# An mLSTM, attention and PEER block on one core: the mLSTM's branch product moved into the attention, and tiles made ahead spread differently

## The chip, the cores and the metric

The kernel runs on one core of a Trainium2 chip. The core has a tensor engine for matrix products (TensorE, PE), a vector engine (VectorE, DVE), a scalar engine for activations (ScalarE, ACT), GpSimd (POOL), and SyncE (SP), whose queue issues most DMA transfers. Each engine works through its own queue in a fixed order and waits on semaphores for what other engines produce. The metric is the device time of one launch in microseconds (us), taken as the median of several runs.

## The reference

One transformer block for 512 latent tokens of width 1024, with 256 context tokens beside them. What matters here, cut to its core:

```
sh1, sc1, g1, sh2, sc2, g2 = adaLN(c) = silu(c) @ w_ada + b_ada          # 6 x 1024 numbers
h = rms(x) * g * (1 + sc1) + sh1
q, k, v, o, gates, aq, ak, av, G = split(h @ w_in)                       # G: two gates of 1024 columns
m = mlstm(q, k, v, gates over latents and context, both directions)       # 4 heads of 128
m = rms(m) * norm_g * sigmoid(o)                                          # 512 columns
a = window_attention(aq, ak, av, context keys, sink)                      # 8 query heads of 64, 2 kv heads
z = sigmoid(G_m) * (m @ w_branch_m) + sigmoid(G_a) * (a @ w_branch_a)
x = x + g1 * (z @ w_out)
x = x + g2 * peer(rms(x) * g * (1 + sc2) + sh2)                           # 16384 experts, 16 of each of 8 heads
```

All is in float32. The two branch products, the gates G and z @ w_out are the part that the change touches; the PEER part (experts) follows and takes most of the time.

## The kernel before

A float32 product is split in three: each operand becomes a high half (a copy rounded by ACT, `whi`, `hhi`) and a low half (the rest, a subtraction, `wlo`, `hlo`), and `mm3` (L182) issues hi times hi, lo times hi and hi times lo into one PSUM bank (L183 to L185). These are called split matmuls below. A product tile gives 128 output columns for all 512 tokens: with an inner width of 1024 it is 24 split matmuls (a gate, `gate_proj`, L646; an output tile), with 512 it is 12 (a branch product).

The part around the change runs in these stages. The projections of h; the mLSTM cell (L480 to L560) over chunks of 128 tokens in both directions; the attention in four blocks of 128 queries (L592 to L643): for a block the scores of eight heads (L607, L608), a masked maximum on DVE (L615), exponentials on ACT (L619), a scaling on DVE (L626), then for each of four or five key blocks eight transposes of the scores (L632), two copies out of PSUM (`pTs`, L635 on DVE, L637 on ACT) and the product with the values (L640, PV). Then `num`, the result of the mLSTM, is transposed (L670) and scaled to `mt` (L672), and split to `mhi`, `mlo`. Sixteen gate tiles of G (L681 and what it calls) are written to a DRAM tile `sgd`. The branch products of both branches follow for eight column tiles (L687 to L713): load the two gate tiles (`sgm`), load and split the weights (`w_br`), 24 split matmuls, two multiplications, one addition on GpSimd, split into `zhi`, `zlo`. Then the output projection with eight tiles of `w_out` (L740 to L753), the norm, and PEER.

The order is not that of the text. A scheduler of the framework lists the instructions of all these stages by priority and readiness and fixes a queue for each engine; so gates are placed between the attention's short operations. It is bounded by buffers: a pool tag with n buffers makes the next tile wait until an earlier one is released. Tag `SGS` (2 buffers) holds the gates, tag `A` (10 slots, `ga`) the large arrays, tag `B` (9) short-lived tiles, `wraw` (4), `whi` and `wlo` (3) the weights. `ps` are PSUM banks for split products.

Three other streams run beside. `adas` (L138) loads weight rows of the adaLN and reduces each with the vector silu(c) in `silp` on DVE (`dot`, L133, 1024 columns; tile `wada`). `ahead(n)` (L355) prepares n tiles of the PEER weights: load (`sraw`, L358), copy to the high half (`shi`, ACT), subtract in place (DVE, L361), and at its next call store the low half in DRAM (`lows`). There are 36 such tiles, and each call site says how many it makes at once. Lines of the kernel before are used above and in the profile; the changed kernel's lines lie 1 to 40 further on in this part.

## Time and profile before

| | us |
|---|---|
| median of 3 runs | 1827.71 (1825.52 to 1828.05) |
| the profiled execution | 1819.1 |
| its span | 1817.3 |
| PE busy in the span | 1736.9 (96%) |
| DVE busy | 1428.5 (79%) |
| ACT busy | 765.2 (42%) |
| GpSimd busy | 487.1 (27%) |

The span runs from the first to the last instruction of one execution, and the profiled execution's time has some 2 us around it. "Busy" is the time in which an engine executes instructions; a matmul's end is modelled and consecutive matmuls overlap, so a busy PE isn't always one at its peak. [...] An idle time is put down to the engine or transfer whose result came last. The rows are in a section of their own below.

### The profile page before, as it was taken

The page shows a single profiled execution, that of the slowest core. Times are in us where ns is not written, and L with a number is a line of the kernel's source. Part 1 is how long each engine was busy: PE and PEld are TensorE (multiplying, and loading weights), DVE is VectorE, ACT ScalarE, POOL GpSimd, SP SyncE. Part 2 cuts the span into 40 slices and gives each one's busy share as a digit, 9 for nine tenths or more (in the row PEclk, how much of TensorE's full clock was granted, in tenths as well). Part 3 has the DMA queues.
Part 4 walks back from the last instruction along what each step waited for, and adds up shares of the span by engine and source line. Part 5 has one row for each costly group of instructions (what it writes and reads, how often), then busy time and mean ns, then how long its engine had stood idle before and what let it go on. Part 6 is the DMA issues. An engine that isn't in the chain of part 4 may idle for free.

```text
span 1817.3 us, 24986 instructions
## 1 busy us (share of the span) xinstructions
PE 1736.9 (96%) x9079; PEld 1479.7 (81%) x9079; DVE 1428.5 (79%) x2756; ACT 765.2 (42%) x1139; POOL 487.1 (27%) x385
## 2 busy tenths in 40 slices
PE   8999898997998999999989999999999999999998
PEld 4877775664777899999889999999999999988886
DVE  6977977454655999999738888888888888886665
ACT  5452466554445334554523333333333333334332
POOL 0001133210203552000025454445454444420000
PEclk9999998998999999999999999999999999999999
DMA  9466645443795225699999999999989999986662
GB/s 370 136 203 197 210 169 182 176 151 116 244 307 181 82 93 208 250 346 345 325 394 375 343 336 352 350 324 355 367 319 353 350 340 340 372 321 249 234 229 81
DMA packets 154764, 485.09 MB, mean 267 GB/s; under 512 B 15376, under 2 KB 45584, under 8 KB 151568
## 3 DMA queue, kind: packets, MB, share of 16 engines
q1 hardware_dynamic: 91088, 314.39, 47.8%
q0 software_dynamic: 37008, 135.28, 20.4%
q10 hardware_dynamic: 26544, 33.82, 5.3%
q8 instruction: 71, 1.16, 0.3%
q14 instruction: 53, 0.43, 0.1%
HBM read 421.30 MB, written 62.13 MB: 266 GB/s over the span
## 4 chain that ended last, share of the span: by engine, by line
PE 70%; DMA 11%; DVE 10%; ACT 5%; issue 3%; POOL 1%; SPq 0%; ACTq 0%; DVEq 0%; POOLq 0%
PE pa L184 9%; PE pa L185 9%; PE pa L183 9%; PE pu L183 9%; PE pu L185 9%; PE pu L184 9%; DMA Gd<-stg 4%; PE ps L185 3%; PE ps L183 2%; PE ps L184 2%; PE a L640 2%; DMA wada<-in_w_adaT 2%; ACT stg L1024 1%; PE a L632 1%; DVE wada L135 1%
## 5 line engine op out<-in xcount | busy, mean ns | idle before, releaser
L183 PE MATMUL pu<-h2hi,whi 128*128 128x384 f32 (+1 forms) x1152 | 402.3, 349 | 4.7 <-ACT St L1134 3.3
L185 PE MATMUL pu<-h2lo,whi 128*128 128x384 f32 (+1 forms) x1152 | 395.9, 344 | 0.7 <-DVE h2lo L180 0.7
L184 PE MATMUL pu<-h2hi,wlo 128*128 128x384 f32 (+1 forms) x1152 | 395.6, 343 | 0.0
L795 DVE TENSOR_TENSOR wlo<-wraw,whi 128x1024 fp32r<-128x1024 f32 x210 | 256.9, 1224 | 99.0 <-ACT whi L784 97.1
L183 PE MATMUL pa<-whi,wh 128*128 128x512 f32 x768 | 299.8, 390 | 5.5 <-ACT wh L1146 5.5
L184 PE MATMUL pa<-whi,wl 128*128 128x512 f32 x768 | 301.6, 393 | 1.8 <-DVE wl L1150 1.7
L185 PE MATMUL pa<-wlo,wh 128*128 128x512 f32 x768 | 301.1, 392 | 0.0
L784 ACT ACTIVATE whi<-wraw 128x1024 fp32r<-128x1024 f32 x272 | 286.5, 1053 | 28.5 <-PE pa L184 10.8
L1071 POOL DMA_INDIRECT gath<-in_u,idx x128 | 166.3, 1299 | 404.4 <-DMA Sd<-St 228.1
L183 PEld LDWEIGHTS pu<-h2hi,whi 128*128 128x128 f32 x1152 | 218.3, 189 | 13.6 <-ACT St L1134 3.6
L184 PEld LDWEIGHTS pu<-h2hi,wlo 128*128 128x128 f32 x1152 | 218.4, 190 | 7.8
L185 PEld LDWEIGHTS pu<-h2lo,whi 128*128 128x128 f32 x1152 | 218.0, 189 | 6.3 <-DVE h2lo L180 1.1
L1071 POOL DMA_INDIRECT gath<-in_v,idx x128 | 164.3, 1284 | 178.4 <-DVE tokh L1103 163.8
L183 PEld LDWEIGHTS pa<-whi,wh 128*128 128x128 f32 x768 | 144.8, 189 | 34.8 <-ACT wh L1146 6.6
L184 PEld LDWEIGHTS pa<-whi,wl 128*128 128x128 f32 x768 | 144.5, 188 | 32.1 <-DVE wl L1150 3.6
L185 PEld LDWEIGHTS pa<-wlo,wh 128*128 128x128 f32 x768 | 144.6, 188 | 30.2
L1103 DVE SCALAR_TENSOR_TENSOR tokh<-gath,gw,tokh 128x1024 f32<-128x1024 f32 x127 | 163.1, 1284 | 0.6
L1146 ACT ACTIVATE wh<-act 128x384 fp32r<-128x384 f32 x84 | 44.2, 526 | 268.7 <-DVE act L1142 268.7
L1095 DVE CUSTOM_DVE_ANT_0 gath<-gath,tokh 128x1024 f32<-128x1024 f32 x128 | 154.6, 1218 | 2.4 <-DMA gath<-in_u,idx 2.4
L1134 ACT ACTIVATE act<-pu 128x384 f32<-128x384 f32 x84 | 41.3, 492 | 178.3 <-PE pu L185 178.3
L52 POOL TENSOR_TENSOR wlo<-wraw,whi 128x1024 fp32r<-128x1024 f32 x20 | 49.0, 2449 | 234.5 <-ACT whi L51 194.8
L51 ACT ACTIVATE whi<-wraw 128x1024 fp32r<-128x1024 f32 (+1 forms) x60 | 61.6, 1028 | 80.8 <-PE ps L184 29.8
(352 smaller groups left out, 2829.2 us busy)
## 6 DMA issues: line engine op xcount, KB each, us to landing
wraw<-in_uT SPq DMA_DIRECT2D x128, 512.0 KB
wraw<-in_v SPq DMA_DIRECT2D x128, 512.0 KB
Gt<-Gd SPq DMA_DIRECT2D x17, 1536.0 KB
Gd<-stg ACTq DMA_DIRECT2D x24, 1024.0 KB
sraw<-in_uT SPq DMA_DIRECT2D x36, 512.0 KB
lows<-sraw SPq DMA_DIRECT2D x36, 512.0 KB
wlo<-lows SPq DMA_DIRECT2D x36, 512.0 KB
wada<-in_w_adaT SPq DMA_DIRECT2D x32, 512.0 KB
```

The costliest lines, as they stand in the source:

```text
L51: S.activation(hi, src, AF.Copy)
L52: (eng or V).tensor_tensor(out=lo, in0=src, in1=hi.bitcast(F32), op=ALU.subtract)
L183: PE.matmul(p, sh, mh, start=first, stop=False)
L184: PE.matmul(p, sl, mh, start=False, stop=False)
L185: PE.matmul(p, sh, ml, start=False, stop=last)
L784: S.activation(his[j], raws[j], AF.Copy)
L795: (G if pool else V).tensor_tensor(out=los[j], in0=raws.pop(j), in1=his[j].bitcast(F32), op=ALU.subtract)
L1071: G.indirect_dma_start(out=t, out_offset=None, in_=sparse["src"][s // 128], in_offset=bass.IndirectOffsetOnAxis(ap=sparse["idx"][:, s // 1 ...
L1095: V.tensor_tensor_reduce(out=t, in0=t, in1=tokh[:, 0], scale=1.0, scalar=0.0, op0=ALU.mult, op1=ALU.add, accum_out=gw[:, 0, s:s + 1])
L1103: V.scalar_tensor_tensor(out=tokh[:, 1], in0=t, scalar=gw[:, 0, s - 128:s - 127], in1=tokh[:, 1], op0=ALU.mult, op1=ALU.add)
L1134: S.activation(acts[i], p, AF.Gelu_apprx_tanh)
L1146: S.activation(wh, acts[i], AF.Copy)
```

## The change

Four things change together. The mLSTM's transposes and `mt` tiles are moved to stand between the first four and the last four gates of the attention's branch, with `mt` in tag `SGS`, and the branch products of the mLSTM are formed beside their gates (for a pair of column tiles at a time) and multiplied into them before the result goes to DRAM. The halves `ahi`, `alo` of the attention's output are made only behind these products; the outputs of the first three blocks wait in `ao` until then. `ahead` is called once beside each gate and each product up to there, then for every second tile in the attention's product and in the output projection. And silu(c) is copied into the mask's tile at the start of the attention, so that the later dots read it there (the name in the order is then `amask`, not `sil`) and the slot of `sil` comes free earlier. The addition of the two branches moves from GpSimd to DVE.

```diff
--- before.py
+++ after.py
@@ -99,6 +99,7 @@
 
     warm = cst.tile([128, 1], F32, name="warm")
     silp = ga([128, 2, D], F32, "sil")
+    sils = [silp[:, 0], silp[:, 1]]
 
     def silu(i, nm):
         nc.sync.dma_start(silp[:, i], A[nm].to_broadcast([128, D]))
@@ -132,7 +133,7 @@
 
     def dot(w, i, col, keep=False):
         junk = wb([128, D], mybir.dt.bfloat16, "junk") if keep else w
-        V.tensor_tensor_reduce(out=junk, in0=w, in1=silp[:, i], scale=1.0, scalar=0.0,
+        V.tensor_tensor_reduce(out=junk, in0=w, in1=sils[i], scale=1.0, scalar=0.0,
                                op0=ALU.mult, op1=ALU.add, accum_out=col)
 
     def adas(a, b):
@@ -562,7 +563,10 @@
     banks(("m2", "m1"), a1=(2, 1), a2=(2, 2))
     aqt = ga([128, NB, 512], F32, "aqt")
     nc.sync.dma_start(aqt, aqd)
-    amask = ga([128, 640], F32, "amask")
+    amask_ = ga([128, 640 + D], F32, "amask")
+    amask = amask_[:, 0:640]
+    S.activation(amask_[:, 640:], silp[:, 0], AF.Copy)
+    sils[0] = amask_[:, 640:]
     nc.sync.dma_start(amask, A["amask"])
     sink = load_const("sink", [128, 8])
 
@@ -588,7 +592,12 @@
         for o in (a, z):
             V.tensor_tensor(out=kst[g][o, 1], in0=pk[a], in1=kst[g][a, 0].bitcast(F32), op=ALU.subtract)
 
-    ahi, alo = ga([128, NB, 4, 128], F32R, "ahi"), ga([128, NB, 4, 128], F32R, "alo")
+    ao = ga([128, 3, 4, 128], F32, "ao")
+    halves = {}
+
+    def attended(n, src):
+        split(halves["ahi"][:, n], halves["alo"][:, n], src)
+
     for n in range(4):
 
         lat = [b for b in (n - 1, n, n + 1) if 0 <= b < 4]
@@ -639,7 +648,8 @@
             for g in range(2):
                 PE.matmul(po[64 * g:64 * g + 64], akv[:, blk, 128 + 64 * g:192 + 64 * g], pts[g],
                           start=(i == 0), stop=(i == nk - 1))
-        split(ahi[:, n], alo[:, n], po)
+        if n < 3:
+            S.activation(ao[:, n], po, AF.Copy)
         adas(28 + 5 * n, 33 + 5 * n)
 
     def gate_tile(name):
@@ -663,23 +673,54 @@
         gate_proj(cO + h * 128, sigo[:, h])
         ahead(1)
     g_m = load_const("g_mlstm", [128, 4])
+
+    sgd = dr.tile([8, 128, 2, T], F32, name="sgd")
+
+    def branch_gate(n, br):
+        st = gen.tile([128, T], F32, name="sgs", tag="SGS", bufs=2)
+        gate_proj(cG + br * 1024 + n * 128, st)
+        return st
+
+    def branch_weights(br, q):
+        wbr = wp.tile([128, 2, 4, 128], F32, name="wraw", tag="wraw", bufs=WR)
+        nc.sync.dma_start(wbr, A["w_br"][br, q])
+        whi = wp.tile([128, 2, 4, 128], F32R, name="whi", tag="whi", bufs=3)
+        wlo = wp.tile([128, 2, 4, 128], F32R, name="wlo", tag="wlo", bufs=3)
+        split(whi, wlo, wbr)
+        return whi, wlo
+
+    def attention_gates(a, b):
+        for n in range(a, b):
+            nc.sync.dma_start(sgd[n, :, 1], branch_gate(n, 1))
+            ahead(1)
+
+    attention_gates(0, 4)
     mhi, mlo = ga([128, NH, T], F32R, "mhi"), ga([128, NH, T], F32R, "mlo")
     for h in range(4):
-        p = pst([128, T], "a1")
+        p = pst([128, T])
         for b in range(4):
             PE.transpose(p[:, b * 128:b * 128 + 128], num[0][:, b, h, 0:128], ident)
-        mt = wb([128, T], F32, "mt")
+        mt = gen.tile([128, T], F32, name="mt", tag="SGS", bufs=2)
         V.scalar_tensor_tensor(out=mt, in0=p, scalar=g_m[:, h:h + 1], in1=sigo[:, h], op0=ALU.mult, op1=ALU.mult)
         split(mhi[:, h], mlo[:, h], mt)
-
-
-    sgd = dr.tile([8, 128, 2, T], F32, name="sgd")
-    for n in range(8):
-        for br in range(2):
-            st = gen.tile([128, T], F32, name="sgs", tag="SGS", bufs=2)
-            gate_proj(cG + br * 1024 + n * 128, st)
-            nc.sync.dma_start(sgd[n, :, br], st)
+    attention_gates(4, 8)
+    for q in range(4):
+        sts = []
+        for i in range(2):
+            sts.append(branch_gate(2 * q + i, 0))
             ahead(1)
+        whi, wlo = branch_weights(0, q)
+        for i in range(2):
+            p = pst([128, T])
+            for k in range(4):
+                mm3(p, whi[:, i, k], wlo[:, i, k], mhi[:, k], mlo[:, k], k == 0, k == 3)
+            V.tensor_tensor(out=sts[i], in0=p, in1=sts[i], op=ALU.mult)
+            nc.sync.dma_start(sgd[2 * q + i, :, 0], sts[i])
+            ahead(1)
+    for nm in ("ahi", "alo"):
+        halves[nm] = ga([128, NB, 4, 128], F32R, nm)
+    for n in range(4):
+        attended(n, ao[:, n] if n < 3 else po)
 
     V.tensor_tensor(out=mod[:, 16:48], in0=mod[:, 16:48], in1=b_ada[:, 16:48], op=ALU.add)
 
@@ -687,31 +728,21 @@
     banks(("a2", "a1", "ps"), ps=(6, 1), ps2=(1, 2))
     zh = [ga([128, 4, T], F32R, "zhi%d" % i) for i in range(2)]
     zl = [ga([128, 4, T], F32R, "zlo%d" % i) for i in range(2)]
-    for n in range(8):
-        sgs = [wb([128, T], F32, "sgm") for _ in range(2)]
-        for br in range(2):
-            nc.sync.dma_start(sgs[br], sgd[n, :, br])
-        wbr = wp.tile([128, 2, 4, 128], F32, name="wraw", tag="wraw", bufs=WR)
-        nc.sync.dma_start(wbr, A["w_br"][n])
-        whi = wp.tile([128, 2, 4, 128], F32R, name="whi", tag="whi", bufs=3)
-        wlo = wp.tile([128, 2, 4, 128], F32R, name="wlo", tag="wlo", bufs=3)
-        split(whi, wlo, wbr)
-        pz = []
-        for br, (ah, al) in enumerate(((mhi, mlo), (ahi, alo))):
+    for q in range(4):
+        whi, wlo = branch_weights(1, q)
+        for i in range(2):
+            n = 2 * q + i
+            sgs = [wb([128, T], F32, "sgm") for _ in range(2)]
+            for br in range(2):
+                nc.sync.dma_start(sgs[br], sgd[n, :, br])
             p = pst([128, T])
             for k in range(4):
-                if br == 0:
-                    mh, ml = ah[:, k], al[:, k]
-                else:
-                    mh, ml = ah[:, :, k], al[:, :, k]
-                mm3(p, whi[:, br, k], wlo[:, br, k], mh, ml, k == 0, k == 3)
-            pz.append(p)
-        z0 = wb([128, T], F32, "sgm")
-        V.tensor_tensor(out=sgs[0], in0=pz[0], in1=sgs[0], op=ALU.mult)
-        V.tensor_tensor(out=sgs[1], in0=pz[1], in1=sgs[1], op=ALU.mult)
-        G.tensor_tensor(out=z0, in0=sgs[0], in1=sgs[1], op=ALU.add)
-        split(zh[n // 4][:, n % 4], zl[n // 4][:, n % 4], z0)
-        ahead(1)
+                mm3(p, whi[:, i, k], wlo[:, i, k], halves["ahi"][:, :, k], halves["alo"][:, :, k], k == 0, k == 3)
+            z0 = wb([128, T], F32, "sgm")
+            V.tensor_tensor(out=sgs[1], in0=p, in1=sgs[1], op=ALU.mult)
+            V.tensor_tensor(out=z0, in0=sgs[0], in1=sgs[1], op=ALU.add)
+            split(zh[n // 4][:, n % 4], zl[n // 4][:, n % 4], z0)
+            ahead(i)
     g1 = mod[:, 16:24]
     x1T = Pair(F32, T, "x1T")
     x1d = dr.tile([128, 4, D], F32, name="x1d")
@@ -750,7 +781,7 @@
         square(x1T, n, acc, T)
         if n:
             residual_out(n - 1)
-        ahead(1)
+        ahead(n % 2)
     ahead(0)
 
 
@@ -1400,7 +1431,8 @@
     f["sink"] = np.tile(a["attn_sink"][0], (128, 1))
     cut = lambda m: m.reshape(-1, 128, m.shape[1] // 128, 128).transpose(2, 1, 0, 3)
     f["w_gate"] = ct(cut(np.concatenate([f["w_in"][:, 2048:2560], f["w_in"][:, 2832:]], axis=1)))
-    f["w_br"] = ct(np.stack([cut(a["w_branch_m"][0]), cut(a["w_branch_a"][0][hp])], 2))
+    pair = lambda m: cut(m).reshape(4, 2, 128, 4, 128).transpose(0, 2, 1, 3, 4)
+    f["w_br"] = ct(np.stack([pair(a["w_branch_m"][0]), pair(a["w_branch_a"][0][hp])]))
     f["w_out"] = ct(cut(a["w_out"][0]))
     f["w_in"] = ct(f["w_in"][:, 0:2832])
     f["w_q"] = ct(a["peer_w_query"][0].reshape(8, 128, 16, 128).transpose(2, 1, 0, 3).reshape(16, 128, 1024))
```

The queue that the scheduler makes for PE changes most. This is the start of the first attention block's PV before; `a` with a number is a PSUM tile, `hhi`, `hlo` the halves of h, so L183 to L185 are matmuls of a gate:

```order
L183 MATMUL ps<-hhi_212,whi 128x512
L184 MATMUL ps<-hhi_212,wlo 128x512
L185 MATMUL ps<-hlo_214,whi 128x512
L632 MATMUL a_2199<-c_ident,sm 128x128
L183 MATMUL ps<-hhi_211,whi 128x512
L632 MATMUL a_2199<-c_ident,sm 128x128 x2
L184 MATMUL ps<-hhi_211,wlo 128x512
L632 MATMUL a_2199<-c_ident,sm 128x128
L185 MATMUL ps<-hlo_213,whi 128x512
L632 MATMUL a_2206<-c_ident,sm 128x128
L183 MATMUL ps<-hhi_211,whi 128x512
L632 MATMUL a_2206<-c_ident,sm 128x128
```

And the same place now, with all of the block's first two key blocks (L641 are the transposes, L649 the PV, L702 the transposes of `num`):

```order
L641 MATMUL a_2199<-c_ident,sm 128x128 x4
L641 MATMUL a_2206<-c_ident,sm 128x128 x2
L649 MATMUL a_2113<-pTs,akv 64x512
L641 MATMUL a_2206<-c_ident,sm 128x128 x2
L649 MATMUL a_2113<-pTs,akv 64x512
L641 MATMUL a_2215<-c_ident,sm 128x128 x4
L702 MATMUL ps<-c_ident,num_1471 128x128 x4
L641 MATMUL a_2222<-c_ident,sm 128x128 x4
L649 MATMUL a_2113<-pTs,akv 64x512
L702 MATMUL ps<-c_ident,num_1471 128x128 x4
L649 MATMUL a_2113<-pTs,akv 64x512
```

Where three matmuls of a gate stood to every two or three transposes, none stands now; the transposes of `num` came from behind the attention. The next matmul of a gate comes 138 instructions after the eighth gate's last.

On DVE the dots have moved. This is the queue at the start of the mLSTM before (`vL`, `kvc` and `ktok` are copies of values and keys, L135 a dot with its read of the sum):

```order
L135 ISA wada_2457,mod<-wada_2457,sil 128x1024
L135 ISA mod 128x1
L135 ISA wada_2460,mod<-wada_2460,sil 128x1024
L135 ISA mod 128x1
L486 COPY vL<-ps 128x4x128 x2
L135 ISA wada_2631,mod<-wada_2631,sil 128x1024
L135 ISA mod 128x1
L486 COPY kvc<-ps 128x4x128
L493 COPY ktok<-ps 128x512 x4
L135 ISA wada_2634,mod<-wada_2634,sil 128x1024
L135 ISA mod 128x1
```

This is the queue in the PV of the first attention block now (L136 a dot, L704 `mt`, L644 copies of transposed scores):

```order
L136 ISA wada_2628,mod<-wada_2628,amask 128x1024
L136 ISA mod 128x1
L644 COPY pTs<-a_2206 128x512
L704 SCALAR_TENSOR_TENSOR mt<-ps,c_g_mlstm,sigo 128x512
L644 COPY pTs<-a_2215 128x512
L704 SCALAR_TENSOR_TENSOR mt<-ps,c_g_mlstm,sigo 128x512
L362 TENSOR_TENSOR sraw<-sraw,shi 128x1024
L136 ISA wada_2631,mod<-wada_2631,amask 128x1024
L136 ISA mod 128x1
L362 TENSOR_TENSOR sraw<-sraw,shi 128x1024
L136 ISA wada_2634,mod<-wada_2634,amask 128x1024
L136 ISA mod 128x1
```

The dots that stood around the copies of keys and values now stand among the copies that the PV needs, with `mt` and the tiles made ahead.

On SP, whose queue issues the loads, these are the weights of the last branch products before (`sgm` loads a gate back from `sgd`, which a store of `sgs` has written):

```order
L695 DMA wraw<-in_w_br 128x1024
L693 DMA sgm<-sgd 128x512 x4
L355 DMA lows<-sraw 128x1024
L358 DMA sraw<-in_uT 128x1024
L693 DMA sgm<-sgd 128x512 x2
L355 DMA lows<-sraw 128x1024
L695 DMA wraw<-in_w_br 128x1024
L693 DMA sgm<-sgd 128x512 x2
```

And those of the attention's product now:

```order
L718 DMA sgd<-sgs 128x512
L737 DMA sgm<-sgd 128x512
L356 DMA lows<-sraw 128x1024
L718 DMA sgd<-sgs 128x512
L359 DMA sraw<-in_uT 128x1024
L686 DMA wraw<-in_w_br 128x1024
L737 DMA sgm<-sgd 128x512 x2
L359 DMA sraw<-in_uT 128x1024
```

The load of weights (L686) now stands among the stores of the last gated products (L718); before, no store of a gate was left in this place.

## Rows read from the trace of the kernel before

**Rows 1.** Part 1 of the page: busy us, share of the span, instructions

```profile
PE 1736.9 (96%) x9079; PEld 1479.7 (81%) x9079; DVE 1428.5 (79%) x2756; ACT 765.2 (42%) x1139; POOL 487.1 (27%) x385
```

**Rows 2.** busy time of each engine by stage; the first line names the columns

```profile
core 0: us, PE busy (x) PEld busy (x) DVE busy (x) ACT busy (x) POOL busy (x), PEclk, DMA share, GB/s
178.00:187.00 9.00, 3.25 (x21) 2.47 (x20) 7.29 (x12) 1.53 (x2) 1.45 (x1) 0.80 0.84 291
187.00:260.00 73.00, 67.86 (x439) 59.52 (x437) 61.60 (x154) 42.98 (x90) 11.84 (x5) 0.98 0.53 184
260.00:285.00 25.00, 20.33 (x85) 15.84 (x85) 21.52 (x21) 14.98 (x20) 14.11 (x4) 0.86 0.37 133
285.00:343.00 58.00, 55.06 (x251) 37.66 (x251) 36.33 (x81) 39.02 (x64) 12.72 (x6) 0.97 0.49 170
343.00:418.40 75.40, 75.40 (x331) 47.54 (x330) 35.38 (x79) 41.10 (x68) 14.15 (x6) 1.00 0.48 170
418.40:445.00 26.60, 20.50 (x50) 6.90 (x50) 11.02 (x18) 8.18 (x11) 0.00 (x0) 0.68 0.39 140
445.00:450.50 5.50, 2.45 (x17) 1.59 (x17) 4.77 (x8) 2.60 (x5) 0.00 (x0) 1.00 0.44 137
450.50:497.00 46.50, 44.88 (x192) 36.02 (x193) 27.99 (x34) 17.84 (x21) 11.96 (x7) 1.00 0.63 220
497.00:552.00 55.00, 50.18 (x221) 38.58 (x220) 31.45 (x34) 25.65 (x32) 2.95 (x3) 1.00 0.89 305
420.00:435.00 15.00, 12.34 (x26) 4.00 (x26) 8.12 (x12) 5.38 (x7) 0.00 (x0) 0.58 0.54 189
```

**Rows 3.** timeline of PE, 429 to 451: start, us, line, names [idle before, releaser]

```profile
429.81 1.97 PE L640 MATMUL a<-pTs,akv 128*64 128x512 f32 x2
...
434.37 1.12 PE L632 MATMUL a<-c_ident,sm 128*128 128x128 f32 x4
...
450.50 0.47 PE L183 MATMUL ps<-mhi,whi 128*128 128x512 f32 x1 [1.96 <-DVE mt L672]
```

**Rows 4.** timeline of PE, 347 to 349, columns as in rows 3

```profile
347.90 0.60 PE L632 MATMUL a<-c_ident,sm 128*128 128x128 f32 x4
348.43 1.07 PE L640 MATMUL a<-pTs,akv 128*64 128x512 f32 x2
```

**Rows 5.** timeline of PE, 456 to 484, columns as in rows 3

```profile
456.10 0.39 PE L183 MATMUL ps<-mhi,whi 128*128 128x512 f32 x1
...
483.87 0.39 PE L183 MATMUL ps<-mhi,whi 128*128 128x512 f32 x1
```

**Rows 6.** tile wada, 150 to 235: count, ns min/median/max, first and last start

```profile
L135 DVE CUSTOM_DVE_ANT_0 wada<-wada,sil x20: 1205/1221/3471, 150.4 to 218.9; 128x1024 f32<-128x1024 f32 x20
```

**Rows 7.** timeline of PE, 178 to 187, columns as in rows 3

```profile
181.46 1.25 PE L492 MATMUL ps<-c_ident,kT 128*128 128x128 f32 x8 [1.94 <-DVE vL L486]
186.52 0.77 PE L504 MATMUL m<-qT,kT 128*128 128x128 f32 x2 [3.81 <-DVE ktok L493]
```

**Rows 8.** timeline of DVE, 179 to 184, columns as in rows 3

```profile
179.57 1.22 DVE L135 CUSTOM_DVE_ANT_0 wada<-wada,sil 128x1024 f32<-128x1024 f32 x1 [2.36 <-DMA wada<-in_w_adaT]
```

**Rows 9.** groups of DVE, 285 to 445: busy us, mean ns, idle before

```profile
L615 DVE CUSTOM_DVE_ANT_0 sm<-a,amask,c_sink 128x640 f32<-128x640 f32 (+1 forms) x24 | 19.4, 835 | 1.7 <-PE a L608 1.7
L361 DVE TENSOR_TENSOR sraw<-sraw,shi 128x1024 fp32r<-128x1024 f32 x14 | 19.4, 1388 | 18.5 <-ACT shi L360 18.5
L626 DVE TENSOR_SCALAR sm<-sm,mx 128x512 f32<-128x512 f32 (+1 forms) x32 | 16.2, 580 | 0.1
...
L617 DVE TENSOR_SCALAR mx<-mx 128x1 f32<-128x1 f32 x32 | 4.4, 147 | 0.0
```

**Rows 10.** groups of DVE, 450.5 to 552, columns as in rows 9

```profile
L52 DVE TENSOR_TENSOR wlo<-wraw,whi 128x1024 fp32r<-128x1024 f32 x13 | 17.4, 1339 | 8.2 <-ACT whi L51 8.0
...
L52 DVE TENSOR_TENSOR zlo<-sgm,zhi 128x512 fp32r<-128x512 f32 x8 | 5.5, 689 | 11.6 <-ACT zhi L51 11.6
```

**Rows 11.** DMA queues, 497 to 552: packets, MB, share of 16 engines

```profile
q1 hardware_dynamic: 8060, 16.76, 89.2%
```

## The prediction, made before the changed kernel was run

> **What bounds the kernel now.** I read the page's busy shares first: TensorE (PE) is busy 96% of the span [rows 1], so a change pays where PE waits or runs at a low clock, and costs where it opens such a place. Then I cut the stretch the diff touches into its stages and read a table by stage [rows 2]; before 178 us and behind 552 us the instructions stand in the old order, so these 374 us decide. Three of its stages have gaps: 178 to 187 us (PE busy 3.25 of 9), 418.4 to 445 (20.50 of 26.6, granted clock 0.68) and 445 to 450.5 (2.45 of 5.5). From 343 to 418.4 PE is busy all the time at a clock of 1.00: there one split matmul after another of the gates lies between the attention's short chains. [...] So the question for the change is where the 480 split matmuls of this stretch (288 of gates, 192 of products) stand: the price of one is the time from 456.10 to 483.87, which 120 of them fill, 0.2314 us each [rows 5].
>
> **Start of the mLSTM, 178 to 285.** Twenty adaLN dots (VectorE, DVE, 1.22 us each) ran from 150.4 to 218.9 [rows 6]; eleven of them lie behind 178 us. Their weight tiles came early because the vector `sil` held a slot that others wait for; now a copy in the mask's tile serves them, and the order has them late: seven at the end of the mLSTM and thirteen in the first two attention blocks. At the start PE waits 1.94 us for the value copies and 3.81 for the key copies [rows 7]; in front of each stands a dot in DVE's queue, and the first dot waited 2.36 us for its transfer [rows 8]. I take two dots and a third of that wait, -3.2 us (0 to -5.75). From 187 to 260 PE idles 5.1 of 73 and DVE loses its remaining dots: -2 (0 to -5). From 260 to 285 seven dots, 8.5 us, come to a DVE that has 3.5 of 25 free, with PE idle 4.7 already: +2.5 (0 to +8.5). Sum -2.7. The nine dots before 178 stood beside dense matmuls and are counted at nothing.
>
> **First uncovered stretch, 285 to 343.** The four `mt` tiles of the mLSTM now use the two buffers that gates use (tag SGS), ahead of the next gates. The order shows what follows: after the eighth gate (285 us) PE's queue holds no split matmul until the fourth `mt` is made, in the PV of the second block. Before, 128 of them lay there, and PE was busy 55.06 of 58 at 0.97 [rows 2]; these 29.6 us of work go behind. What is left is the serial chain of blocks one and two, as in the old tail. Without cover I price a key block of PV like the tail, 26.6 / 4 = 6.65 us, less the tail's 1.00 us of start shared by four: 6.4. The chain from 285: two dots, two `sraw` subtractions (1.39 each) and eight scalings (0.58 each) with 2 us of exponentials and sums [rows 9], 12 us; four key blocks, 25.6; the scores of block two, eight times 0.835 + 0.147 [rows 9], 7.9; two dots, eight scalings and the small operations, 8.5; one key block, 6.4. Together 60.4 us where 58 stood, and reads of the accumulators on top: +3. The thirteen dots of this stretch are part of it only where they are named; the others lie where DVE waits for PE. Bounds: at a full clock a key block is 2 x 0.60 + 2 x 1.0 and two waits of 0.75, 4.7, or 3.2 if the waits overlap, so five of them save 8.5 to 16; upward, if the other nine dots all add, +11.
>
> [...] The row: with 12.34 of 15 us busy on transposes and PV, PE was granted 0.58 [rows 2]. [...]
>
> **Second block to the end of attention, 343 to 445.** Before: 101.95 us, with 160 split matmuls and the bare tail. Now 186 split matmuls lie there and reach the tail. The tail's own work at a full clock is 8 x 0.60 + 8 x 1.0 = 12.8 us instead of 26.6 (-13.8); 26 more split matmuls add 6.0; the clock must rise first, +1.5 by my estimate from the clock of 0.97 in neighbouring stages. Sum -6.3 (-10 to 0). Of the mLSTM's branch product only two of eight tiles (24 of 96 matmuls) stand beside the attention: the rest stands behind it, which is why the saving isn't larger.
>
> **mt stage, 445 to 450.5.** It goes: its transposes and scalings are in the stretch above. PE's wait of 1.96 us for the last mt goes with it [rows 3]. -5.5; what is late next is the split of the fourth block's output, hidden behind gates.
>
> **Gates and products, 450.5 to 497.** Before: 192 split matmuls, 46.5 us [rows 2]. Now 198 behind the attention (gates of the mLSTM branch with six product tiles) and 96 of the attention's product: 294 x 0.2314 = 68.0, +21.5. This pays for the 128 that left the first stretch.
>
> **Lateness in these stages.** In the last 96 matmuls (22.2 us) DVE has eight multiplications, eight additions that GpSimd did before, eight splits, 0.69 each, with six `wlo` at 1.34 [rows 10] and five `sraw` at 1.39, as [rows 9] have it: 31.6 us. PE can run ahead into the output projection only by the `k` whose halves are made, about 5 us. I take +6.5 (0 to +12). DMA: a round of two gates and two products (72 matmuls, 16.7 us) moves eleven tiles of 512 KB and two of 256, 6.3 MB or 377 GB/s; the row gives 16.76 MB at a share of 89.2% over 55 us, which is 342 at a full share [rows 11]. The 2.75 rounds would take 50.5 us instead of 45.8. The low-half stores can lag, and the loads of weights have four buffers: 0 (0 to +5). In SP's queue the weights of the attention's product now stand behind the stores of the last gated products, which wait for PE; I count that in the 6.5.
>
> [...]
>
> **Output projection, 497 to 552.** 54.7 us against 192 x 0.2314 = 44.4, with `wlo` as what PE waits for. Three ahead tiles instead of six stand there, each a load, a store, 1.22 us of DVE: I take -6 (-9 to 0).
>
> **Sum.** -2.7 + 3 - 6.3 - 5.5 + 21.5 + 6.5 + 0 - 6 = +10.5 against the profiled execution's 1819.1 us (span 1817.3), 1829.6. The runs shown have a median of 1827.71, 8.6 above the profiled execution, so the forecast is 1827.7 + 10.5, some 1838 us. A measurement here tells 0.2% (3.7 us) from no change.
>
> **Rivals.** One: the clock stays up in the bare stretch. For it: between 285 and 343 the clock was 0.97, and the granted clock of 187 to 260 was 0.98 with short operations among the split ones [rows 2]. Against it: the 0.58 of the tail, which has the same instructions. Then the term is -10 instead of +3 (a key block 3.2 to 4.7 instead of 6.4): the sum is -2.5, 1825 us, not slower, with 1822 at its lower end. It decides if the granted clock there is over some 0.85.
> Two: the late stages are bound by DMA and DVE together. For it: 377 GB/s wanted against 342, 31.6 us of DVE beside 22.2 of PE, and a share of 0.89 in the projection behind [rows 2, 11]. Against it: the share of 0.63 in the old products. Lateness becomes 5 + 12 and the sum +21: 1849 us.
> Three: the end overlaps well (lateness 0, projection at -8) and the start gives 6: -6 + 3 - 6.3 - 5.5 + 21.5 - 8 = -1.3, 1826 us, no measurable change. For it: PE needs only the first `k` halves to start the projection; against it: DVE's order is fixed, and seven dots move into the mLSTM's end.
> That the product isn't beside the attention at all is half true by the order (six of eight tiles) and is in the sum.
>
> **How the numbers follow.** Forecast (1832 to 1844) 0.42, rival one 0.20, two 0.18, three 0.20. Faster by over 0.2%: two fifths of rival one and a third of rival three, 0.15. Within 0.2%: the rest of both and a little of the forecast's edge, 0.22. Slower: 0.63. The range goes from rival one's lower part to rival two's middle, 1823 to 1849.
>
> **What would show it.** Right: between 285 and some 345 us a granted clock near 0.6 and PE idle over 10 us, with no `hhi` matmul; a clock of 1.00 through the rest of the attention; no transposes of `num` behind it; the first matmul of the projection some 15 us later than now. Wrong: a first stretch under 52 us (rival one), a last product stage over 34 us or weights waited for from DMA (rival two), a projection under 47 us right behind a 22 us product stage (rival three). A mLSTM that ends later than 285 by over 5 us would mean that the seven dots cost more than I counted.

## The result and the profile after

The changed kernel is slower: 1838.11 us (median of 7 runs) against 1823.53, a ratio of 1.0074 with a 95% interval of 1.0050 to 1.0098. That is +14.6 us where +10.5 was forecast. That the forecast time, 1838 us, was met to within 1 us is luck: with four more runs the median of the kernel before came out 4.2 us lower than the 1827.7 that the forecast started from, and the change 4.1 us larger. The profiled executions (1819.1 and 1837.57 us) lie 4.4 below and 0.5 below these medians, so their spans differ by 18.5 us. Each term can be read in them.

First the table by stage of the changed kernel, columns as in [rows 2]; the bounds are the same places in the program. The clock (column PEclk) is the mean clock granted to PE in a stretch, as a share of its full speed. In the trace of before it was 1.00 from 420 to 422 us and 0.50 from 424 to 438; these two are the upper and the lower level below.

```profile
150.00:176.00 26.00, 26.00 (x121) 21.33 (x121) 5.68 (x19) 6.04 (x12) 4.78 (x2) 1.00 0.25 88
...
176.00:275.10 99.10, 88.32 (x540) 75.27 (x538) 83.89 (x169) 56.67 (x108) 23.59 (x8) 0.98 0.43 151
275.10:334.30 59.20, 42.00 (x149) 22.25 (x150) 49.85 (x108) 27.04 (x52) 7.29 (x3) 0.77 0.58 199
334.30:428.40 94.10, 93.01 (x395) 55.80 (x394) 49.30 (x106) 49.75 (x79) 12.45 (x5) 0.98 0.37 130
...
428.40:483.20 54.80, 48.41 (x199) 37.94 (x198) 22.96 (x21) 22.60 (x25) 9.67 (x4) 0.97 0.79 270
483.20:514.20 31.00, 25.85 (x96) 19.88 (x96) 20.17 (x26) 11.76 (x14) 0.00 (x0) 0.89 0.93 313
514.20:571.20 57.00, 50.03 (x221) 39.98 (x221) 33.04 (x35) 25.37 (x33) 7.14 (x3) 0.97 0.78 266
...
320.00:335.00 15.00, 10.38 (x26) 4.74 (x27) 12.55 (x29) 4.75 (x12) 0.00 (x0) 0.62 0.42 141
```

Beside the stages of before, with what was forecast:

| stage | before us | after us | difference | forecast |
|---|---|---|---|---|
| to the eighth gate (285.05; 275.1) | | | -10.0 | -2.7 |
| bare stretch | 58.2 | 59.2 | +1.0 | +3 |
| rest of the attention | 101.8 | 94.2 | -7.6 | -6.3 |
| mt stage | 5.5 | none | -5.5 | -5.5 |
| product stages | 46.5 | 85.7 | +39.2 | +21.5 and +6.5 |
| output projection to the norm | 56.9 | 57.0 | +0.1 | -6 |
| sum | | | +17.2 | +10.5 |

Then rows with a wait from PE's timeline, columns as in [rows 3].

```profile
179.31 1.13 PE L505 MATMUL m<-qT,kT 128*128 128x128 f32 x8 [1.52 <-DVE ktok L494]
...
325.24 2.39 PE L641 MATMUL a<-c_ident,sm 128*128 128x128 f32 x5 [3.46 <-DVE sm L635]
327.78 1.97 PE L649 MATMUL a<-pTs,akv 128*64 128x512 f32 x2 [0.16 <-ACT pTs L646]
...
468.03 0.50 PE L184 MATMUL ps<-hhi,whi 128*128 128x512 f32 x1 [1.63 <-ACT whi L51]
470.51 0.79 PE L185 MATMUL ps<-hhi,wlo 128*128 128x512 f32 x1 [1.98 <-POOL wlo L52]
...
493.60 0.74 PE L184 MATMUL ps<-ahi,whi 128*128 128x512 f32 x2 [3.74 <-ACT whi L51]
...
516.57 0.50 PE L184 MATMUL ps<-zhi,whi 128*128 128x512 f32 x1 [2.40 <-ACT whi L51]
```

The wait for keys fell from 3.81 to 1.52 us [rows 7]. The bare stretch looks like the old tail (before, the fourth block's PV from 418.4 us on, with the gates used up): PV pairs of 1.97 us [rows 3], a clock of 0.62 in its last 15 us, 0.77 over all. New are waits for halves of weights in the product stages, which were nearly dense before (44.88 of 46.5 us busy [rows 2]).

### The profile page after: what moved, and what is told of

Same layout as the page of the kernel before. It is cut to its first block, busy times and chain, and to the rows that moved or that the text cites. A ratio compares the mean times of both kernels' runs of the same rounds, so it can differ in the third digit from the quotient of the medians.

```text
span 1835.8 us, 24969 instructions
## 1 busy us (share of the span) xinstructions
PE 1741.5 (95%) x9079; PEld 1481.8 (81%) x9079; DVE 1437.8 (78%) x2764; ACT 762.8 (42%) x1139; POOL 473.9 (26%) x377
## 4 chain that ended last, share of the span: by engine, by line
PE 59%; DMA 8%; DVE 5%; ACT 3%; issue 1%; POOL 0%; SPq 0%; ACTq 0%; DVEq 0%; POOLq 0%
PE pa L185 9%; PE pa L186 9%; PE pa L184 9%; PE pu L184 9%; PE pu L186 9%; PE pu L185 9%; DMA Gd<-stg 5%; PE ps L185 1%; PE ps L186 1%; ACT stg L1055 1%; PE ps L184 1%; PE pg L911 1%; DMA wraw<-in_v 1%; ACT whi L815 1%; PE pg L1048 1%
## 5 line engine op out<-in xcount | busy, mean ns | idle before, releaser
L185 PE MATMUL pu<-h2hi,wlo 128*128 128x384 f32 (+1 forms) x1152 | 395.4, 343 | 0.0
L185 PE MATMUL pa<-whi,wl 128*128 128x512 f32 x768 | 301.4, 393 | 2.2 <-DVE wl L1181 2.1
L184 PEld LDWEIGHTS pu<-h2hi,whi 128*128 128x128 f32 x1152 | 218.1, 189 | 13.7 <-ACT St L1165 3.7
L185 PEld LDWEIGHTS pu<-h2hi,wlo 128*128 128x128 f32 x1152 | 218.4, 190 | 7.8
L185 PEld LDWEIGHTS pa<-whi,wl 128*128 128x128 f32 x768 | 144.5, 188 | 32.5 <-DVE wl L1181 3.9
L52 POOL TENSOR_TENSOR wlo<-wraw,whi 128x1024 fp32r<-128x1024 f32 x20 | 50.6, 2528 | 311.5 <-ACT whi L51 254.6
L826 POOL TENSOR_TENSOR wlo<-wraw,whi 128x1024 fp32r<-128x1024 f32 x26 | 62.4, 2398 | 165.9 <-ACT whi L815 165.9
## 6 DMA issues: line engine op xcount, KB each, us to landing
Gd<-stg ACTq DMA_DIRECT2D x24, 1024.0 KB, 10.5
```

Source lines behind the costliest of these rows:

```text
L52: (eng or V).tensor_tensor(out=lo, in0=src, in1=hi.bitcast(F32), op=ALU.subtract)
L184: PE.matmul(p, sh, mh, start=first, stop=False)
L185: PE.matmul(p, sl, mh, start=False, stop=False)
L826: (G if pool else V).tensor_tensor(out=los[j], in0=raws.pop(j), in1=his[j].bitcast(F32), op=ALU.subtract)
```

## The experiments

Twelve kernels ran, each beside the kernel before; ratios are against it. The stages are read from one profiled execution of each kernel. "First score" is when the first score starts, "attention" the us from there to the end of the last PV, "product stages" the us from there to the last matmul of the attention's product, with the number of split matmuls that the order puts there and the excess, which is the us less 0.2314 for each of these matmuls; "projection" goes from there to the norm. In before and in dots late alone, the mt stage (5.5 us before) is part of the product stages and so of the excess.

| kernel | ratio (95%) | first score | attention | product stages: us, matmuls, excess | projection |
|---|---|---|---|---|---|
| before | 1 | 266.5 | 178.4 | 52.3, 192, 7.9 | 56.7 |
| changed | 1.0074 (1.0050 to 1.0098) | 256.4 | 172.1 | 85.7, 294, 17.7 | 57.0 |
| dots late alone | 1.0008 (0.9989 to 1.0028) | 257.3 | 183.1 | 60.2, 220, 9.3 | 54.7 |
| dots early | 1.0049 (1.0028 to 1.0069) | 266.1 | 159.9 | 72.0, 284, 6.3 | 62.5 |
| eight gates first | 1.0005 (0.9988 to 1.0022) | 254.5 | 177.4 | 60.3, 221, 9.2 | 55.4 |
| tiles early | 1.0098 (1.0073 to 1.0123) | 254.7 | 182.6 | 72.2, 309, 0.7 | 59.9 |
| stores by GpSimd | 1.0165 (1.0141 to 1.0189) | 257.3 | 170.1 | 85.0, 295, 16.7 | 66.8 |
| eight gates, dots early | 1.0008 (0.9991 to 1.0025) | 265.2 | 180.0 | 45.9, 192, 1.5 | 65.0 |
| the same, tiles spread | 0.9947 (0.9929 to 0.9966) | 265.7 | 163.4 | 52.2, 221, 1.1 | 60.3 |
| bare attention | 1.0382 (1.0338 to 1.0425) | 258.5 | 174.2 | 133.9, 480, 22.8 | 55.8 |
| tiles late | 1.0081 (1.0052 to 1.0110) | 257.1 | 173.6 | 76.2, 294, 8.2 | 60.8 |
| half loads | 1.0059 (1.0037 to 1.0081) | 255.5 | 171.3 | 74.7, 293, 6.9 | 63.0 |
| eight gates, tiles spread, dots late | 0.9940 (0.9917 to 0.9962) | 261.6 | 173.2 | 52.1, 221, 1.0 | 57.8 |
| eight gates, dots early, spread, GpSimd adds | 0.9977 (0.9961 to 0.9992) | 266.6 | 166.5 | 52.2, 221, 1.1 | 64.8 |

### What the dots do

**Dots late alone**: the kernel before with `amask_`, `S.activation(amask_[:, 640:], silp[:, 0], AF.Copy)` and `sils`, as in the diff, and nothing else.

> The kernel before, with only the copy of silu(c) into the mask's tile (the twenty dots go late). Theory: the 10 us by which the changed kernel is ahead at the eighth gate (275.1 us instead of 285.05) come from these dots alone, which leave the start of the mLSTM; nothing else of the change stands ahead of that place. Then this kernel has the eighth gate at 275 to 278 us. Its order keeps 28 gate matmuls behind the attention (+6.5) and gives the old tail 25 of them and a higher clock (-10), so about 14 us under before, some 1810. Rival A: the gain comes from the moved mt and gates, not from the dots: eighth gate at 285 us and 1823 within 4. Rival B: the thirteen dots cost in the attention what they gain ahead of it: eighth gate at 276, but 1820 to 1826.

**Dots early**: the changed kernel without those lines.

> The changed kernel with the dots back at their early place (no copy of silu(c)). Theory: the front loses the 10 us again (eighth gate near 285 us); the bare stretch is partly covered, since the order has 24 gate matmuls in the first block's PV, and ten fewer stand behind the attention: together +4 to +9 against the changed kernel, 1842 to 1847. Rival A (front gain not from the dots): 1838 or less, eighth gate at 275.

```profile
266.10:426.00 159.90, 144.08 (x605) 87.52 (x606) 95.40 (x197) 81.66 (x140) 28.28 (x10) 0.96 0.37 130
426.00:498.00 72.00, 68.43 (x285) 54.05 (x285) 37.35 (x39) 31.70 (x36) 9.57 (x4) 0.98 0.84 304
```

The rows are of the kernel with early dots, columns as in [rows 2]. The front's 9 to 10 us are the dots' (257.3 with them late alone), but they don't reach the end: late alone they change the time by nothing that is measured. 4.7 us go in the attention and 7.9 in the product stages, where 28 matmuls more stand (6.5 us). Rival B of the first was right about the time, in part about the place, and the theory's 1810 us was wrong. In the changed kernel I had expected 4 to 9 us more without the move; the ratio is 1.0049, which excludes that. It is under 1.0074, but the two intervals overlap, so that the move is a loss there isn't shown. In the profiled executions the attention is 12.2 us shorter without it and the product stages 13.7, with ten matmuls and two tiles made ahead fewer in them, the projection 5.5 longer.

### What the wall of mt costs

**Eight gates first**:

```diff
-    attention_gates(0, 4)
+    attention_gates(0, 8)
...
-    attention_gates(4, 8)
```

> The changed kernel with all eight gates of the attention's branch written ahead of the mt tiles instead of four. Its order has 130 more gate matmuls up to the first third of the second block's PV, and 73 fewer behind the attention. Theory: the wall of mt in the gates' two buffers is what opened the bare stretch; with it gone the granted clock of the first two blocks is over 0.95 instead of 0.77, and 73 x 0.2314 = 17 us less stand behind the attention: 1838 - 17 = 1821. Rival: the stages behind are bound by loads of weights and tiles made ahead, whatever PE has to do there, so that the attention grows by what is put in it and the end is not earlier: 1834 to 1840.

**Bare attention**:

```diff
-        mt = gen.tile([128, T], F32, name="mt", tag="SGS", bufs=2)
+        mt = wb([128, T], F32, "mt")
```

> The changed kernel with mt in a short-lived tile of tag B, as before, where it waits for the attention's scores to go: the order then has no split matmul at all from the first block's PV to the end of the attention, 288 gate matmuls behind it. It measures the bare attention. Theory: without cover PE is granted the lower clock, and a key block of PV takes some 6 us; 18 of them and four times 18 us for scores and softmax make 180 us from the first score to the last PV, as long as with the cover (172), at a granted clock under 0.7, and 480 - 238 = 242 more matmuls stand nowhere else: about 190 x 0.2314 = 55 us over the changed kernel or more, near 1890. Rival: the clock stays up without cover and a key block takes 3.2 to 4.7 us: 140 us for the attention, some 1850.

Windows of eight gates first (two rows, from the first score), then of the bare attention (the whole, its end, and the stages behind it):

```profile
254.50:432.00 177.50, 160.46 (x672) 100.97 (x673) 128.26 (x231) 93.69 (x151) 35.18 (x13) 0.94 0.55 188
432.00:492.10 60.10, 54.38 (x222) 42.84 (x223) 35.33 (x38) 26.82 (x31) 4.78 (x2) 0.94 0.88 307
```

```profile
258.50:432.70 174.20, 129.09 (x405) 60.81 (x406) 98.49 (x204) 55.10 (x108) 17.31 (x6) 0.75 0.25 86
335.00:432.70 97.70, 73.73 (x210) 29.35 (x210) 35.60 (x93) 23.94 (x52) 0.00 (x0) 0.71 0.03 9
432.70:566.50 133.80, 119.91 (x489) 94.85 (x489) 60.14 (x64) 56.49 (x65) 21.39 (x9) 0.95 0.78 275
```

With one call moved nearly the whole loss is gone (1.0005 instead of 1.0074): the attention is 5 us longer and holds the gates that were missing, the stages behind are 25 shorter, 16.9 by their 73 matmuls and the rest by less lateness (four tiles fewer are made ahead in them). The bare attention, 1887.56 us where 1890 was expected, shows the price: its 52 split matmuls all stand ahead of 278 us, behind them the clock is low (0.71 from 335 us on), DMA idles at the end, and yet the attention is as long as that of the changed kernel with 187 matmuls more (174.2 and 172.1 us). There they cost nothing; behind the attention the same matmuls cost 48.2 us, their 0.2314 us each and 5 us of lateness. It is a balance and no rule, since they take PE's time and the clock is higher with them (0.90 against 0.75 over the attention): with 245 split matmuls and early dots it takes 159.9 us, with 337 (eight gates, dots early) 180.0.

### What makes the product stages late

**Tiles early** (two tiles beside each gate of the attention's branch, none beside the mLSTM's products) and **tiles late** (none there, one more beside every second tile of the two later loops):

```diff
-            ahead(1)                     # attention_gates
+            ahead(2)                     # only in: tiles early
...
-            ahead(1)                     # beside the mLSTM's products, in both
...
-            ahead(i)                     # attention's product
+            ahead(1)                     # only in: tiles late
...
-        ahead(n % 2)                     # output projection
+        ahead(1)                         # only in: tiles late
```

> The changed kernel with two tiles made ahead beside each gate of the attention's branch and none beside the products of the mLSTM's branch (36 in all as before). Theory: of the 17.8 us by which the two product stages (428.4 to 514.2 us) exceed their 294 matmuls, 9.0 us in the first come from waits for weights that queue behind the tiles made ahead in the four raw buffers; with eight tiles fewer there it takes 3 us over its matmuls instead of 9. The last product stage keeps its 8.8. The gates in the attention wait for buffers more (the order has 10 matmuls more behind the attention, +2.3), and the first block is covered by some 24 fewer. Sum -6 + 2 + 2, 1836. Rival: the stage is late by DMA bandwidth or by DVE, so that fewer tiles there give back all of 9 and also start the next stage early: 1826. Second rival: the raw buffers now hold up the gates in the attention: 1845.

> The changed kernel with eight tiles made ahead fewer beside the products of the mLSTM's branch, and four more each beside the attention's product and the output projection. PE's order is the same up to the products. Theory: the tiles made ahead are what makes the product stages late (85.7 us for 294 matmuls of 68.0): the first stage, 54.8 us, comes down to 47, the second (31.0) stays within 2 with twice the tiles, and the output projection goes from 57 to 60. Sum -5, 0.25% under the changed kernel. Rival: the lateness is not theirs but that of the chain from gate to product to store, and the first stage keeps its 54.8: no change or 2 to 4 us slower.

**Stores by GpSimd**: `nc.gpsimd.dma_start(lows[i - P0], lo)` instead of `nc.sync`.

> The changed kernel with the stores of the low halves issued from GpSimd's queue instead of SP's; the same tiles, bytes and buffers, and nearly the same PE order (one matmul differs). In the changed kernel SP waited 34.4 us in the two product stages with a store of a low half at its head, and the loads of weights stand behind it. Theory 1: it is this order in SP's queue that makes the weights late; without it the stages (85.7 us, 17.7 over their matmuls) lose at least 10 us: 1828. Theory 2: it is the four raw buffers, which a tile made ahead keeps from its load to the end of its store; then nothing changes: 1838 within 3. Theory 3: DMA bandwidth: nothing changes either, but the share of the queues is over 0.95 wherever PE waits.

**Half loads**:

```diff
-            nc.sync.dma_start(raw, A["uT"][i].rearrange("p k n -> p (k n)"))
+            nc.sync.dma_start(raw[:, 0:512], A["uT"][i].rearrange("p k n -> p (k n)")[:, 0:512])
...
```

The lines left out make the high half twice from the half that was loaded and the low half zero. The subtractions then take 1.40 us each, against 1.30 in the same stages of the changed kernel.

> The changed kernel, with half of each tile made ahead loaded (256 KB instead of 512), its high half made twice from that half, its low half zero (so these tiles' values are left out); the same instructions on ACT and DVE, the same buffers, the same stores. Of the 24.5 MB that the two product stages move, 12 loads of 0.26 MB go, 3.1 MB. Theory 1: DMA bandwidth makes the stages late: 21.4 MB at 342 GB/s are 62.6 us, less than the matmuls' 68, so the stages take 70 to 74 us instead of 85.7 and the kernel is 12 us faster than the changed one. Theory 2: the four raw buffers do (a tile made ahead keeps one through load, copy, subtraction and store): a shorter load frees them 1 to 2 us sooner of some 12, so the stages keep 13 us or more of their 17.7.

SP's longest waits in the product stages of the changed kernel (engine, line, what it waited for: us, times, longest):

```profile
SPq L356 <- DVE sraw L362: 34.4, 15, 5.5
SPq L718 <- DVE sgs L717: 11.8, 6, 3.2
```

The same with the stores by GpSimd:

```profile
SPq L359 <- DMA lows<-sraw: 16.1, 5, 5.3
SPq L686 <- DMA lows<-sraw: 10.0, 5, 3.5
```

What PE and ACT waited for there, in the same form: two rows of PE and one of ACT of the changed kernel, two of PE with the stores by GpSimd, one of PE and one of ACT with half loads.

```profile
PE ps L184 <- ACT whi L51: 5.4, 2, 3.7
PE ps L185 <- POOL wlo L52: 4.7, 3, 2.0
ACT shi L361 <- DMA sraw<-in_uT: 26.8, 8, 9.1
...
PE ps L184 <- ACT sgs L668: 6.0, 2, 3.8
PE ps L184 <- DVE sgs L717: 5.3, 3, 4.0
...
PE ps L184 <- DVE sgs L719: 4.0, 2, 2.2
ACT shi L363 <- DMA sraw<-in_uT: 13.8, 6, 4.3
```

Windows of tiles early, both product stages:

```profile
437.30:486.30 49.00, 49.00 (x214) 39.84 (x213) 16.40 (x16) 18.25 (x21) 9.57 (x4) 1.00 0.67 236
486.30:509.60 23.30, 22.52 (x97) 18.34 (x98) 16.95 (x20) 11.38 (x14) 0.00 (x0) 1.00 0.97 339
```

Of tiles late, the same stages:

```profile
430.60:476.20 45.60, 45.60 (x199) 37.02 (x198) 15.18 (x15) 17.66 (x21) 9.58 (x4) 1.00 0.60 214
476.20:506.90 30.70, 26.17 (x97) 19.71 (x96) 21.61 (x26) 13.21 (x16) 0.00 (x0) 0.89 0.92 323
```

Of half loads, both product stages together:

```profile
427.00:501.60 74.60, 69.86 (x294) 56.05 (x294) 41.48 (x40) 34.29 (x39) 9.60 (x4) 0.98 0.81 274
```

Both product stages together of the changed kernel, then of eight gates, dots early:

```profile
428.40:514.20 85.80, 74.26 (x295) 57.82 (x294) 43.13 (x46) 34.35 (x39) 9.67 (x4) 0.94 0.84 286
...
445.20:491.10 45.90, 45.06 (x193) 35.97 (x193) 25.83 (x28) 19.48 (x22) 2.42 (x1) 1.00 0.88 309
```

Of the changed kernel's excess of 17.7 us PE idled 11.5; the other 6.2 are matmuls that took longer than 0.2314 us each, at a clock of 0.94. In three kernels the excess falls with the tiles made ahead in these stages: 17.7 us with 15, 8.2 with 11, 0.7 with 8. But it was 6.3 with 13 in dots early, and 1.5 in eight gates, dots early, where 8 tiles in 45.9 us stand as close as 15 in 85.7: their number alone doesn't give it, nor does the rate of DMA, which is higher in that dense stage (309 GB/s, a share of 0.88) than in the late ones (286, 0.84).

The place of the low-half stores in SP's queue doesn't give the length either: with the stores off it the stages stay at 85.0 us. PE's waits for weights are gone there, but waits for the readers of its product tiles (`sgs`, 11.3 us) have come in their place, and SP waits at its head for the stores themselves to end, before loads of tiles (16.1 us) and of branch weights (10.0), since the four raw buffers are full. The stores of the gated products (L718), which stood at SP's head for 11.8 us and which the prediction had named, were not moved by any run.

Half the bytes of the tiles' loads take 11 us off the stages (74.7 us, a little over theory 1's 70 to 74 and far under theory 2's bound). So a large part of the excess comes from these loads; whether by the bytes, the buffers or ACT isn't separated. The stages move 20.5 MB instead of 24.5, at 274 GB/s instead of 286. ACT copies the tiles in its own fixed order, with copies of weights behind them, and stood 26.8 us at such copies for their loads in the changed kernel, 13.8 with half loads. Whether a buffer comes free sooner with them isn't shown. PE's longest wait in these stages, 3.74 us at 493.60, is for a copy of weights that ACT began at 492.50, after 9.1 us at such a copy of a tile. Of the 6.9 us of excess that half loads leave, PE idles 4.7, none of it for weights and 4.0 of it for the gated products on DVE.

The time doesn't follow the stage, though. Tiles early lose in the attention what they win behind it: it takes 182.6 us, with six tiles more in it, 15 split matmuls fewer and a clock of 0.85 over all, 0.79 from 335 to 359 us; which of these does it isn't shown. Tiles late and half loads win 9.5 and 11 us in the product stages and give back 3.8 and 6 in the projection, and their ratios lie within the changed kernel's interval.

### The version that beats both

**Eight gates, dots early** joins two edits above; **tiles spread** adds: no tile beside the mLSTM's products, `ahead(2)` beside the four output gates (L674), `ahead(1)` beside each tile of the projection. Then the same with dots late, and the first with `G.tensor_tensor` for the addition (L743).

> All eight gates of the attention's branch ahead of mt, and the dots at their early place. The runs so far: late dots gain 9 to 10 us up to the first score and lose 12 from there to the last PV (159.9 us without, 172.1 with them). Theory: DVE is what the attention's chain waits for, so dots in it cost more than at the mLSTM's start, with cover too; the order also has 29 fewer gate matmuls behind the attention (-6.7). Against a_g8: +10 - 10 - 7, ratio to before 0.996, some 8 us less than before. Rival: with cover the dots are hidden in the attention, and the early place costs its 10 us: ratio 1.002.

> As a_g8n, but no tile made ahead beside the products of the mLSTM's branch; one more beside each of the four output gates, and one beside each tile of the output projection (36 in all). Theory: tiles made ahead make the product stages late (15 tiles: 17.7 us, 8 tiles: none), and the output projection takes 55 to 57 us with four or with eight of them. So the late stages lose 5 to 8 us more than in a_g8n: ratio to before 0.992. Rival: the same tiles then make the output projection late: no difference to a_g8n.

> As a_g8xn, but with the dots late, in the attention, as in the changed kernel. Theory: DVE paces the attention (it is as long without cover as with it, 174 and 172 us in the runs so far), so each of the dots there adds its 1.3 us, as much as it gave at the mLSTM's start: the first score comes 9 us sooner, the attention takes 10 to 14 us longer, and the kernel is 0 to 5 us slower than a_g8xn (ratio to before 0.995 to 0.998). Rival: with cover on PE the dots are hidden there, and this kernel is 8 us faster than a_g8xn (0.990).

> As a_g8xn, but the addition of the two gated products is on GpSimd again, as before the change. In a_g8xn the attention's product takes 22.5 us, no longer than its matmuls, but PE then waits 6.5 us in the output projection for the high halves of z, which come from the chain multiplication, addition, split; the projection takes 60.4 us. Theory: DVE paces that chain (31.6 us of its work beside 22.2 us of PE), and eight additions of 0.69 us off it let the projection start 3 to 5 us sooner: 57 us, ratio to before 0.992 to 0.993. Rival: the addition takes 1.8 us on GpSimd and lies in the chain from product to split itself, or the chain waits for the gates' reload from DRAM (4.4 us in a_g8xn): the projection stays at 60 us or more, ratio 0.995.

Windows of eight gates, dots early, tiles spread: attention, product stages, projection.

```profile
265.70:429.10 163.40, 152.66 (x666) 97.37 (x666) 97.84 (x199) 90.32 (x147) 32.17 (x12) 0.97 0.40 136
429.10:481.20 52.10, 51.32 (x223) 41.55 (x223) 26.38 (x29) 21.99 (x26) 4.80 (x2) 1.00 0.70 244
481.20:541.60 60.40, 51.31 (x222) 39.74 (x220) 37.09 (x42) 27.31 (x36) 4.83 (x2) 0.94 0.85 300
```

The product stages are dense, and the kernel takes 0.9947 of before, somewhat more than the 0.992 expected: with mt out of the gates' way and the tiles spread so, the idea pays. It doesn't pay where I expected it, in the product stages, which were as dense without the spread (an excess of 1.5 us, and 1.1 with it): the attention is 16.6 us shorter, with 31 matmuls fewer in it, and the projection 4.7. With late dots the product stages do gain by the spread (60.3 us against 52.1 at 221 matmuls). Where the dots stand then makes no difference (0.9940 and 0.9947): 4 us earlier at the first score, 10 longer in the attention, 2.5 shorter in the projection; the rival's 8 us gain is excluded, and theory's loss isn't seen. Early dots without the spread (1.0008) missed their 0.996: the attention is 17 us longer than with it, with twelve tiles made ahead in its last 100 us where the spread leaves five in 86. The addition on GpSimd loses, more than its rival said: 1.4 us each instead of 0.69, PE waits as long (6.7 us) for the halves of z, and the projection is 4.5 us longer. That the kernel could do better there isn't shown.

## Why the prediction was right

The direction, the time and the main mechanism held; three terms were off by more than they should, and partly cancel (-7.3, +11.2, +6.1).

- **The wall of mt and the bare stretch** (+3; +1.0 measured): right, and so was its clock, 0.62 at the end and 0.77 over all where 0.6 was expected. Rival one is out for this kernel: its 0.77 is under the 0.85 that was to decide, and the bare attention was granted 0.71 over 97.7 us. So transposes and PV alone did not keep the clock up there. The +3 was an estimate from the old tail: 26.6 us for four key blocks, granted 0.58 in its middle [rows 2]. The runs don't part transposes from PV, nor either from the gaps between them (PE was busy 73.73 of the 97.7 us). But the rival isn't out everywhere: with early dots the order has no split matmul from 284.3 to 326.6 us, and the first block's PV ran at the upper level (1.00 from 305 to 315 us) for its last three key blocks, with a pair of PV matmuls at 1.07 us and four transposes at 0.66. A key block then takes some 5 us, near the 4.7 that the prediction estimated for a full clock, with groups of 0.60 and 1.0 us much as in [rows 4]. What decides between the two levels in such a stretch isn't shown. The first row is of the kernel with early dots as in [rows 2], the others are from its PE timeline.

```profile
305.00:315.00 10.00, 6.62 (x25) 2.44 (x24) 1.38 (x2) 1.20 (x2) 0.00 (x0) 1.00 0.32 107
...
308.23 1.07 PE L645 MATMUL a<-pTs,akv 128*64 128x512 f32 x2 [0.74 <-ACT pTs L642]
310.91 0.66 PE L637 MATMUL a<-c_ident,sm 128*128 128x128 f32 x4 [1.02 <-ACT pTs L642]
313.40 1.07 PE L645 MATMUL a<-pTs,akv 128*64 128x512 f32 x2 [0.84 <-DVE pTs L640]
```

- **Rest of the attention and mt stage** (-6.3, -5.5; -7.6, -5.5): right. No `num` transposes stand behind it, and the clock was 0.98.
- **294 matmuls behind instead of 192** (+21.5): right, and shown to be the main cause, by eight gates first.
- **The start of the mLSTM** (-2.7; -10.0): the gain was sized too small, the cost of the seven dots about right. Of the gain 2.6 us stands ahead of the mLSTM, where the nine dots beside dense matmuls were "counted at nothing": PE's clock there was 0.94 before (150 to 178.5 us) and 1.00 after (150 to 176). From there to a matmul late in the mLSTM (250.4 us before, 233.9 now) PE idles 2.9 us instead of 10.1, -7.2 where -5.2 was forecast, and its clock is 1.00 instead of 0.95. The changed kernel is 16.5 us ahead there, but only 10.1 at the first score: six of the seven late dots lie between, and PE waits 1.80 and 2.02 us for results that stand in DVE's queue behind two of them. The same two waits are in dots late alone and in eight gates first, and before PE waits at most 0.78 us in this stretch. PE idles 3.95 us in this stretch instead of 1.14, +2.8 where +2.5 was forecast; the rest of the lost lead is the time of 18 more matmuls in it. The first rows are of before, then come those of the changed kernel.

```profile
150.00:178.50 28.50, 28.06 (x124) 23.30 (x125) 17.53 (x37) 6.81 (x13) 4.53 (x2) 0.94 0.66 216
178.50:250.40 71.90, 61.79 (x404) 54.55 (x403) 61.77 (x151) 38.36 (x79) 10.41 (x5) 0.95 0.57 197
250.40:266.50 16.10, 14.96 (x85) 11.61 (x84) 13.18 (x21) 12.00 (x24) 4.78 (x2) 1.00 0.40 148
...
175.90:233.90 58.00, 55.12 (x382) 49.13 (x381) 43.75 (x124) 34.37 (x75) 7.08 (x3) 1.00 0.32 118
233.90:256.40 22.50, 18.55 (x103) 14.91 (x101) 21.68 (x35) 16.10 (x27) 5.61 (x3) 1.00 0.63 220
...
241.44 3.31 DVE L136 CUSTOM_DVE_ANT_0 wada<-wada,amask 128x1024 f32<-128x1024 f32 x1
245.01 0.49 PE L522 MATMUL m<-vL,dm 128*128 128x129 f32 x2 [1.80 <-DVE num L525]
249.09 3.37 DVE L136 CUSTOM_DVE_ANT_0 wada<-wada,amask 128x1024 f32<-128x1024 f32 x1
252.85 0.87 PE L578 MATMUL a<-c_ident,akv 128*128 128x128 f32 x6 [2.02 <-DVE num L525]
```

- **Lateness** (+6.5; 39.2 - 21.5 = 17.7): the step that failed. It took DVE's 31.6 us beside the last 96 matmuls as the limit and DMA at nothing, "the low-half stores can lag". The traces show otherwise: in tiles early these 96 matmuls take 23.3 us with the same additions on DVE and `ahead` called as often beside them, and the first product stage, taken as not late, was 9.0 over. In place of DVE's work the runs show the loads of tiles made ahead, half of whose bytes are worth 11 us; by which of the ways named above they delay PE stays open, and so does what the rest of the excess comes from. Rival two had the place and the size (17), the size by luck: of its two limits DVE's work is out by the same stage of tiles early, and DMA's rate alone by the dense stages of eight gates, dots early (309 GB/s at an excess of 1.5 us).
- **Output projection** (-6; +0.1): wrong. Fewer tiles there do not shorten it: it took 56.7 us with eight tiles before and 57.0 with four, and 54.7 to 66.8 in all kernels, with no relation to their number that the runs show. Where the product stages are dense, as with the spread tiles, PE waits some 6.5 us here for the halves of z. DVE's work doesn't set that wait: DVE is busy 12.27 of the first 18.8 us there, and with the additions off it PE waits as long (6.7 us).

## What to carry to other kernels

The attention here, a chain of short operations, took 174.2 us bare and 172.1 with 187 split matmuls more in it; behind it the same matmuls cost 48.2 us. But with early dots it took 159.9 us with 245 and 180.0 with 337 (eight gates, dots early). So count which matmuls leave such a chain, since each cost 0.2314 us or more behind it here, and look in the order for a tile that stands in the buffer ring of the filler. Stages where DMA idles (a share of 0.37 in the second half of the attention here) look like the place for prefetches, but the attention was longer where more of them stood in it, in tiles early (182.6 us against 172.1 in the changed kernel) and in eight gates, dots early against the spread (180.0 and 163.4); what else differs there wasn't separated. A gain at one place is real only if the whole time keeps it: two of the gains here, 9.2 us at the first score (dots late alone) and 11 us in the product stages (half loads), don't show in it.
